# Gates of two mixing branches as seven block products ahead of the attention, and attention heads that overlap at their ends

## The chip, the core and the metric

The kernel runs on one core of a Trainium2 chip. The metric is the time of one execution in device microseconds (us). A core has five engines with an instruction stream each: TensorE (PE in the profile) multiplies matrices, VectorE (DVE) and ScalarE (ACT) work elementwise, GpSimd (POOL) copies, fills and issues some transfers, SyncE (SP) issues most transfers. Each engine takes its instructions in order and waits on semaphores for the others.

## The reference

Two layers, each a feed-forward half step, a gated mixing of three branches, and another feed-forward half step, on 512 tokens of 1024 features in float32. The change is in the mixing:

```
u = _rmsnorm(h, mix_pre_g[l])
proj = u @ w_in[l]
q_sb, k_sb, v_sb, q_fx, k_fx, v_fx, f_logit, q_mem = jnp.split(proj, split_at, axis=-1)
o_sb  = _stick_breaking_attention(...)      # 8 heads of 64
o_fx  = _forgetting_attention(...)          # 8 heads of 64
o_mem = _memory_attention(...)              # 4 heads of 128
g_sb, g_fx, g_mem = jnp.split(jax.nn.sigmoid(u @ w_gate[l] + b_gate[l]), N_BRANCH, axis=-1)
merged = (g_sb * (_merge_heads(o_sb) @ w_br_sb[l])
          + g_fx * (_merge_heads(o_fx) @ w_br_fox[l])
          + g_mem * (_merge_heads(o_mem) @ w_br_mem[l]))
h = h + _rmsnorm(merged @ w_out[l], mix_post_g[l])
```

Both causal attentions multiply queries by keys (scores `z`), turn them to weights by chains of exponentials, and multiply these by the values.

## The kernel before

Every matrix product in float32 is done as three matmuls (`mm3`, L212-216). Each factor is split into a high half, a cast on ACT (L188, or L191 with a scale), and the rest, a subtraction on DVE (L189, L192); the product is high x high, high x low and low x high. Tiles with an h or l in the name (`wh_`, `wl_`) are these halves.

A weight unit (`Unit`) is half a megabyte: SP loads it into a `raw` buffer (L262; four buffers), ACT and DVE split it into a `wh` and a `wl` tile (four of each, used in a ring). Work for PE is kept as jobs in a queue `Q`; a job loads its units, and units of later jobs are loaded and split ahead. Attention heads are generators ("chains") that `Q.weave` interleaves with jobs: a chain yields the PE time it has emitted and a time that it wants to wait, and jobs fill the waits. So the order of the program is set by these written times, and the engines follow it.

The feed-forward parts use a scheme of block products in place of the plain one: a product of 2 x 2 blocks by 2 x 2 blocks is done as seven products (n = 0 to 6) with sums of blocks as factors. Such units are `BlockUnit`s: products 2 and 5 have a sum of two weight blocks, built in a buffer `kt` by one load on SP and an adding load on POOL (L317); products 3 and 6 add a third block to the same buffer on DVE (L343). Factors on the token side that are sums are `ag_2` to `ag_5`. The `kt` buffers of the feed-forward groups are of the tag `v`, which has six.

In the mixing part of a layer `us_a` holds the normalised tokens, already split. Order: keys and values of the memory (`pmk`, `pmv`), queries of the memory heads (`pqm_0` to `pqm_3`, tile `qm`), four memory heads (scores `zm`, transposes `ptm`, values `pvm`), then for each pair of heads the projections (`pq`, `pk`, `pv`) and eight stick-breaking heads (scores `zs`, weights `ts`, transposes `pts`, values `pvs`, branch 0), and eight forgetting heads (`zf`, `pf`, `ptf`, `pvf`, branch 1). What fills the waits is merging: for each branch and quarter of the features `merge` runs the gate's product (bank `pg`, weights `wg`), the sigmoid as a chain of five steps on ACT and DVE (tile `ga`, L202-210), the branch's own product (bank `pb`, weights `wb`), and adds to `mg`. Gates are computed directly before they are used, with 512 tokens as the moving side:

```
pg = pbank("mm", "pg" + nm)
products = gemm(pg[:], ug, m, act)
```

## Time and profile before

| | |
|---|---|
| runs, us | 2353.73, 2354.14, 2354.50 (median 2354.14) |
| profiled execution, span from first to last instruction, us | 2352.7 |
| instructions | 30543 |
| TensorE busy, us | 2342.4 |
| VectorE busy, us | 1779.2 |
| ScalarE busy, us | 1453.0 |
| GpSimd busy, us | 213.4 |
| bytes moved, mean | 366.46 MB, 156 GB/s |

The profiled execution is known by its span alone; the runs, which take in what lies ahead of the first and behind the last instruction, are 1.0 to 1.8 us longer. Busy times are sums of the rows of an engine. A matmul's row lasts from its issue to the modelled end of its result, and the next is issued before that, so rows overlap; what a stream of matmuls costs is read from the distance of their starts. In group rows the columns are line, engine, operation, output and inputs, shape and count, then busy us and mean ns of one, then idle time of the engine just before and what ended it. In rows of a timeline they are start and length in us. Wait rows give the engine, its instruction, what it waited for, us in total, times, and the longest.

### The profile page before, as it was taken

What the parts mean: (1) busy time and instruction counts of PE and PEld (TensorE: products, weight loads), DVE (VectorE), ACT (ScalarE), POOL (GpSimd) and SP (SyncE); (2) the same over time, 40 slices, a digit from 0 to 9 for tenths busy, and PEclk for the clock granted to TensorE, in tenths of its full rate; (3) what the DMA queues carried; (4) which work ended last, traced back from release to release, by engine and by line L of the source; (5) the groups of instructions that cost most, each with busy time, mean ns of one, the idle gap of its engine ahead of it and who ended that gap; (6) DMA issues with size and microseconds to landing.
All of it is one profiled execution on the core that took longest, in us unless ns stands there. A gap on an engine that the chain in (4) does not pass through costs nothing.

```text
span 2352.7 us, 30543 instructions
## 1 busy us (share of the span) xinstructions
PE 2342.4 (100%) x11368; PEld 1970.4 (84%) x11368; DVE 1779.2 (76%) x2423; ACT 1453.0 (62%) x2347; POOL 213.4 (9%) x242
## 2 busy tenths in 40 slices
PE   9999999999999999999999999999999999999998
PEld 8888888888888888888888888888888888888887
DVE  8766977678776687768887679766877766866696
ACT  6665765576665565566665566656776655655574
POOL 1101100001120011101011110000011100111100
PEclk9999999999999999999999999999999999999999
DMA  8866854222323476659586767532222234776682
GB/s 249 234 180 173 230 181 142 72 73 81 88 66 116 153 221 173 179 158 258 174 215 170 187 186 232 190 101 81 72 82 81 72 126 153 223 182 176 179 224 98
DMA packets 233112, 366.46 MB, mean 156 GB/s; under 512 B 11242, under 2 KB 101634, under 8 KB 232452
## 3 DMA queue, kind: packets, MB, share of 16 engines
q1 hardware_dynamic: 202400, 305.76, 40.2%
q0 software_dynamic: 30560, 58.76, 14.5%
q8 instruction: 89, 1.46, 0.3%
q14 instruction: 59, 0.48, 0.1%
q10 hardware_dynamic: 4, 0.00, 0.0%
HBM read 349.80 MB, written 14.68 MB: 155 GB/s over the span
## 4 chain that ended last, share of the span: by engine, by line
PE 60%; DVE 0%; issue 0%; ACT 0%; DVEq 0%
PE ptc L214 5%; PE ptc L216 5%; PE ptc L215 5%; PE pdc L214 3%; PE pdc L216 3%; PE pdc L215 3%; PE pta L214 3%; PE pta L216 3%; PE pta L215 3%; PE pg L214 2%; PE pg L215 2%; PE pg L216 2%; PE pda L215 2%; PE pda L216 2%; PE pda L214 2%; PE pb L216 1%
## 5 line engine op out<-in xcount | busy, mean ns | idle before, releaser
L214 PE MATMUL pg<-us_a,wh_wg 128*128 128x512 f32 x384 | 150.9, 393 | 0.0
L216 PE MATMUL pg<-us_a,wl_wg 128*128 128x512 f32 x384 | 149.6, 390 | 0.0
L215 PE MATMUL pg<-us_a,wh_wg 128*128 128x512 f32 x384 | 149.5, 389 | 0.0
L189 DVE TENSOR_TENSOR wl_tc<-ktc,wh_tc 128x1024 fp32r<-128x1024 f32 x80 | 97.7, 1224 | 63.6 <-ACT wh_tc L188 63.6
L189 DVE TENSOR_TENSOR wl_ta<-kta,wh_ta 128x1024 fp32r<-128x1024 f32 x80 | 97.6, 1224 | 58.4 <-ACT wh_ta L188 58.4
L188 ACT CAST wh_tc<-ktc 128x1024 fp32r<-128x1024 f32 x80 | 84.1, 1054 | 68.0 <-PE ptc L216 47.8
L216 PE MATMUL pta<-wh_ta,aga 128*128 128x512 f32 x320 | 124.7, 390 | 1.2 <-DVE aga L189 1.2
L214 PE MATMUL ptc<-wh_tc,agc 128*128 128x512 f32 x320 | 125.4, 393 | 0.1
L214 PE MATMUL pta<-wh_ta,aga 128*128 128x512 f32 x320 | 125.2, 392 | 0.0
L216 PE MATMUL ptc<-wh_tc,agc 128*128 128x512 f32 x320 | 124.7, 390 | 0.0
L215 PE MATMUL ptc<-wl_tc,agc 128*128 128x512 f32 x320 | 124.6, 389 | 0.0
L188 ACT CAST wh_ta<-kta 128x1024 fp32r<-128x1024 f32 x80 | 84.2, 1053 | 65.5 <-PE pta L216 41.7
L215 PE MATMUL pta<-wl_ta,aga 128*128 128x512 f32 x320 | 124.6, 389 | 0.0
L189 DVE TENSOR_TENSOR wl_tc<-raw_tc,wh_tc 128x1024 fp32r<-128x1024 f32 x56 | 68.5, 1224 | 45.4 <-ACT wh_tc L188 45.4
L189 DVE TENSOR_TENSOR wl_ta<-raw_ta,wh_ta 128x1024 fp32r<-128x1024 f32 x58 | 70.9, 1224 | 42.0 <-ACT wh_ta L188 41.9
L188 ACT CAST wh_ta<-raw_ta 128x1024 fp32r<-128x1024 f32 x58 | 60.9, 1052 | 45.6 <-PE pta L216 38.0
L188 ACT CAST wh_tc<-raw_tc 128x1024 fp32r<-128x1024 f32 x56 | 59.0, 1054 | 48.1 <-PE ptc L216 36.6
L214 PE MATMUL ptc<-wh_tc,us_b 128*128 128x512 f32 x224 | 87.6, 391 | 0.2
L214 PE MATMUL pda<-wh_da,aa 128*128 128x512 f32 x224 | 87.5, 391 | 0.0
L214 PE MATMUL pdc<-wh_dc,ac 128*128 128x512 f32 x224 | 87.5, 391 | 0.0
L216 PE MATMUL ptc<-wh_tc,us_b 128*128 128x512 f32 x224 | 87.2, 389 | 0.0
L215 PE MATMUL ptc<-wl_tc,us_b 128*128 128x512 f32 x224 | 87.2, 389 | 0.0
(559 smaller groups left out, 7417.1 us busy)
## 6 DMA issues: line engine op xcount, KB each, us to landing
raw_wg<-in_w_gate_dram SPq DMA_DIRECT2D x48, 512.0 KB, 3.6
raw_ta<-in_ffn_w_gate_dram SPq DMA_DIRECT2D x44, 512.0 KB, 4.3
raw_tc<-in_ffn_w_gate_dram SPq DMA_DIRECT2D x44, 512.0 KB, 4.6
raw_da<-in_ffn_w_down_dram SPq DMA_DIRECT2D x42, 512.0 KB, 3.9
raw_dc<-in_ffn_w_down_dram SPq DMA_DIRECT2D x42, 512.0 KB, 3.9
kta<-in_ffn_w_up_dram SPq DMA_DIRECT2D x40, 512.0 KB, 6.1
ktc<-in_ffn_w_up_dram SPq DMA_DIRECT2D x40, 512.0 KB, 5.7
raw_wo<-in_w_out_dram SPq DMA_DIRECT2D x24, 512.0 KB, 3.7
```

The costliest lines, as they stand in the source:

```text
L188: both = [nc.scalar.copy(h_ap, src)]
L189: make = lambda: nc.vector.tensor_tensor(l_ap, src, h_ap.bitcast(F32), ALU.subtract)
L214: nc.tensor.matmul(pt, lh, rh, start=start, stop=False, skip_group_check=free)
L215: nc.tensor.matmul(pt, lh, rl, start=False, stop=False, skip_group_check=free)
L216: nc.tensor.matmul(pt, ll, rh, start=False, stop=stop, skip_group_check=free)
```

## The change

For branches 0 (stick-breaking) and 1 (forgetting) the gate is no longer computed at the merge. The product `w_gate` x tokens is done as seven block products, features on the output's partitions and 256 tokens on the moving side (`block_gates`). Product 0 of both branches and product 1 of branch 0 stand ahead of the memory queries, the rest (2 to 6 of branch 0, then 2, 3, 4, 5, 1, 6 of branch 1) behind them and ahead of the causal heads. `settle` takes the sigmoid with ACT's own function (which needs an activation table of its own, loaded there and put back behind) and stores the gate to DRAM (`gsave`, a DMA of ACT's queue); `merge` reads it back by a DMA of POOL's queue. The memory branch's gate stays as it was (`mem_gate`), and its own product stands in a job apart (`mem_branch`). The factors `ag_2`, `ag_3` are tiles of the tag `tri`, `ag_4h`, `ag_4l`, `ag_5h`, `ag_5l` of the tag `o`, as are the sums of weight blocks `kt`; `o` has eight buffers, as before. `block_units`, `seeds` and the token sums (`input_sums`) were moved to the top, so that both users share them.

The causal heads are one chain (`causal`): when a head has emitted its transposes, the next head's chain is started 3 us later (`W_NEXT`), so that its scores stand ahead of the previous head's values. The table of extra waiting times by head (`W_MORE`) is gone.

```
+        def factor(n):
+            if n < 4:
+                t = stile([P, 2, 4, S // 2], "tri", f"ag{l}_{n}")
+                return t[:, 0], t[:, 1]
+            return tuple(stile([P, 4, S // 2], "o", f"ag{l}_{n}{x}")[:] for x in "hl")
...
+        def settle(br, i, j, banks=None):
+            t = st.pop(("c", i, j))
+            for m in range(4):
+                c = HALVES[m % 2]
+                d = br * ND + 4 * j + m
+                nc.scalar.activation(t[:, m // 2, c], t[:, m // 2, c] if banks is None else banks[m // 2][:, c], AF.Sigmoid,
+                                     bias=nbgate[:, l, d:d + 1], scale=-1.0 if j else 1.0)
+            nc.scalar.dma_start(gsave[br, i, j], t[:].rearrange("p e q -> p (e q)"))
+
+        def block_gates(br, n, uns, top):
...
+            if n in (0, 1, 2) and not seeded:
+                st["gb", SUM[n]] = [pbank("mm", f"{nm}_{n}_{e}") for e in range(2)]
+            pts = st.pop(("gb", 1)) if n == 1 else st["gb", SUM[n]]
+            opens, ends = n in (0, 1, 2) and not seeded, n in (1, 4, 6)
+            for un in uns:
+                for k in range(un.nk):
+                    kk = un.k0 + k
+                    for m in range(4):
+                        c = slice(m * P, (m + 1) * P)
+                        mm3(pts[m // 2][:, HALVES[m % 2]], un.h[:, k, c], un.l[:, k, c], *tokens(n, kk),
+                            opens and kk == 0 and m % 2 == 0, ends and kk == ND // 2 - 1 and m % 2 == 1, free=True)
+                        yield 3 * S // 2 * PE_US
...
+            for e in range(2):
+                if n in (2, 3):
+                    nc.scalar.copy(t[:, e], pts[e][:])
+                elif n in (4, 5):
+                    nc.vector.tensor_tensor(t[:, e], t[:, e], pts[e][:], ALU.add)
...
+            if n not in (2, 3):
+                settle(br, i, j, None if n in (4, 5) else pts)
...
-                    if br == 2:
-                        nc.vector.tensor_tensor(md, a[:], pb[:], ALU.mult)
-                    else:
-                        nc.vector.tensor_tensor(a[:], a[:], pb[:], ALU.mult)
-                        nc.vector.tensor_tensor(md, md, a[:], ALU.add)
+                    nc.vector.tensor_tensor(a[:], a[:], pb[:], ALU.mult)
+                    nc.vector.tensor_tensor(md, md, a[:], ALU.add)
...
+        todo, made = [], None
+        for br, order in zip(SETS, (FIRST, ORDER)):
+            keep = Keep(lambda i, k0, br=br: stile([P, 2, S], "o", f"kt{l}_{br}_{i}_{k0}", F32)[:])
+            made, rounds = block_units(order, keep, ND // 2, f"wg{l}_{br}", w_gate[l][:, br * D:(br + 1) * D], made)
+            top = max((1, 4), key=order.index)
+            todo.append([(uns, lambda br=br, n=n, uns=uns, top=top: block_gates(br, n, uns, top)) for n, uns in rounds])
+        Q.add(*todo[0].pop(0), src.ready((0, 1)))
+        Q.add(*todo[0].pop(0))
+        Q.add(*todo[1].pop(0))
...
+            def causal(n):
...
+                for kind, us_ in begun.pop(n, None) or head_of(n):
+                    yield kind, us_
+                    steps += kind == "pe"
+                    if kind == "pe" and steps == 2 and n + 1 < 2 * NH:
+                        Q.spawn(causal(n + 1), W_NEXT)
```

How the instructions stand now. TensorE behind the last memory queries, in layer 0: before, the first head's projection and the memory heads follow (`pqm_3` is the last query product, `pvm_0` the values of the first memory head):

```order
L216 MATMUL pqm_3_3477<-us_a_1_3056,wl_qm_1_4_3278 128x512
L214 MATMUL pq_0_0_3552<-us_a_0_3055,wh_q_0_0_3313 128x512
L215 MATMUL pq_0_0_3552<-us_a_0_3055,wh_q_0_0_3313 128x512
L216 MATMUL pq_0_0_3552<-us_a_0_3055,wl_q_0_0_3314 128x512
L214 MATMUL pvm_0_3556<-ptm_0_3516,mv_0_3307 128x512
```

Now the products of the gates stand there first. This is TensorE where branch 0 goes over to branch 1 (`g_0_0` and `g_1_2` are banks by branch and sum; `wh_wg_1_3_0` is the weight unit of branch 1, product 3, first half):

```order
L216 MATMUL g_0_0_1_3705<-us_a_1_3057,wh_wg_0_6_2_3834 128x256
L217 MATMUL g_0_0_1_3705<-us_a_1_3057,wh_wg_0_6_2_3834 128x256
L218 MATMUL g_0_0_1_3705<-us_a_1_3057,wl_wg_0_6_2_3835 128x256
L216 MATMUL g_1_0_0_4034<-ag_3_3611,wh_wg_1_3_0_3959 128x256
L217 MATMUL g_1_0_0_4034<-ag_3_3611,wh_wg_1_3_0_3959 128x256
L216 MATMUL g_1_0_1_4035<-ag_3_3611,wh_wg_1_3_0_3959 128x256
L217 MATMUL g_1_0_1_4035<-ag_3_3611,wh_wg_1_3_0_3959 128x256
L216 MATMUL g_1_2_0_4038<-ag_2_3528,wh_wg_1_2_0_3895 128x256
L217 MATMUL g_1_2_0_4038<-ag_2_3528,wh_wg_1_2_0_3895 128x256
```

Four matmuls of product 3 of branch 1 come directly behind product 6 of branch 0, and product 2 behind them. VectorE at the same place: before, splits of the value weights and work of the memory heads:

```order
L189 TENSOR_TENSOR wl_v_0_2_3432<-raw_v_0_2_3281,wh_v_0_2_3431 128x1024
L189 TENSOR_TENSOR qm_3_3549<-pqm_3_3477,qm_3_3549 128x512
L189 TENSOR_TENSOR om_0_3385<-pvm_0_3556,om_0_3385 128x512
L1386 TENSOR_REDUCE stm_2_0_3572<-zm_2_0_3565 128x2
L1386 TENSOR_REDUCE stm_2_1_3588<-zm_2_1_3581 128x2
```

Now (`cg` collects a quarter of the gates; L1622 empties a bank into it; L345 adds the third block to the sum):

```order
L191 TENSOR_TENSOR wl_wg_0_6_0_3828<-kt_0_0_0_3326,wh_wg_0_6_0_3827 128x1024
L1622 TENSOR_TENSOR cg_0_01_3823<-cg_0_01_3823,g_0_2_0_3708 128x512
L1622 TENSOR_TENSOR cg_0_01_3823<-cg_0_01_3823,g_0_2_1_3709 128x512
L191 TENSOR_TENSOR wl_wg_0_6_2_3835<-kt_0_0_2_3329,wh_wg_0_6_2_3834 128x1024
L1622 TENSOR_TENSOR cg_0_11_3758<-cg_0_11_3758,g_0_0_0_3704 128x512
L191 TENSOR_TENSOR wl_wg_1_2_0_3896<-kt_1_0_0_3690,wh_wg_1_2_0_3895 128x1024
L1622 TENSOR_TENSOR cg_0_11_3758<-cg_0_11_3758,g_0_0_1_3705 128x512
L191 TENSOR_TENSOR wl_wg_1_2_2_3900<-kt_1_0_2_3699,wh_wg_1_2_2_3899 128x1024
L345 TENSOR_TENSOR kt_1_0_0_3690<-kt_1_0_0_3690,raw_wg_1_3_0_3693 128x1024
L345 TENSOR_TENSOR kt_1_0_2_3699<-kt_1_0_2_3699,raw_wg_1_3_2_3702 128x1024
```

The split of `kt_0_0_2` for product 6 of branch 0 and the splits of `kt_1_0_0` and `kt_1_0_2` for product 2 of branch 1 now follow each other there. SyncE, behind the loads of the query weights, before:

```order
L262 DMA raw_qm_1_4_3151<-in_w_in_dram 128x4x256
L262 DMA raw_q_0_0_3209<-in_w_in_dram 128x8x128
L262 DMA raw_k_0_0_3215<-in_w_in_dram 128x8x128
L262 DMA raw_v_0_0_3275<-in_w_in_dram 128x2x512
L262 DMA raw_v_0_2_3281<-in_w_in_dram 128x2x512
```

and now, where the buffers of `kt_1_0_0` and `kt_1_0_2` are those that `kt_0_0_0` and `kt_0_0_2` held:

```order
L319 DMA raw_wg_1_3_0_3693<-in_w_gate_dram 128x2x512
L319 DMA raw_wg_1_3_2_3702<-in_w_gate_dram 128x2x512
L319 DMA raw_wg_1_1_0_3831<-in_w_gate_dram 128x2x512
L319 DMA raw_wg_1_1_2_3838<-in_w_gate_dram 128x2x512
L319 DMA kt_1_0_0_3690<-in_w_gate_dram 128x2x512
L319 DMA kt_1_0_2_3699<-in_w_gate_dram 128x2x512
L319 DMA kt_1_1_0_3765<-in_w_gate_dram 128x2x512
L319 DMA kt_1_1_2_3772<-in_w_gate_dram 128x2x512
L264 DMA raw_q_0_0_4026<-in_w_in_dram 128x8x128
L264 DMA raw_k_0_0_4032<-in_w_in_dram 128x8x128
```

The loads of the first head's weights moved behind those of the gates. TensorE between the first two stick-breaking heads, before:

```order
L1278 MATMUL pvs_0_0_4010<-pts_0_0_3959,v_0_0_3780 128x512 x2
L1278 MATMUL pvs_0_0_4010<-pts_0_0_3959,v_0_1_3808 128x384 x2
L1278 MATMUL pvs_0_0_4010<-pts_0_0_3959,v_0_2_3872 128x256 x2
L1278 MATMUL pvs_0_0_4010<-pts_0_0_3959,v_0_3_3909 128x256 x2
L1305 MATMUL zs_0_1_3_4024<-k_0_0_3743,q_0_0_3689 128x512 x2
L1305 MATMUL zs_0_1_2_4025<-k_0_0_3743,q_0_0_3689 128x384 x2
L1305 MATMUL zs_0_1_1_4026<-k_0_0_3743,q_0_0_3689 128x256 x4
```

and now:

```order
L1307 MATMUL zs_0_1_3_5031<-k_0_0_4572,q_0_0_4495 128x512 x2
L1307 MATMUL zs_0_1_2_5032<-k_0_0_4572,q_0_0_4495 128x384 x2
L1307 MATMUL zs_0_1_1_5033<-k_0_0_4572,q_0_0_4495 128x256 x4
L1280 MATMUL pvs_0_0_5067<-pts_0_0_4990,v_0_0_4609 128x512 x2
L1280 MATMUL pvs_0_0_5067<-pts_0_0_4990,v_0_1_4749 128x384 x2
L1280 MATMUL pvs_0_0_5067<-pts_0_0_4990,v_0_2_4837 128x256 x2
L1280 MATMUL pvs_0_0_5067<-pts_0_0_4990,v_0_3_4874 128x256 x2
```

The scores of the second head moved ahead of the values of the first. Lines of the changed kernel are 2 higher at this place (L1305 is now L1307, L262 now L264, L317 now L319, L189 now L191, L343 now L345).

More of the change, by code (lines that the diff above doesn't have):

```diff
@@ L1363, in fox_head @@
             ptile[i] = p
+        ahead()
         yield ("pe", 1.5)
@@ new lines, in merge, with run @@
+        def merge(br, w_br, dp):
+            ub = wpair(w_br[l], NP, dp * 256, f"wb{l}_{br}_{dp}")
+            def run():
+                gate = []
+                for m in range(2):
+                    d = 2 * dp + m
+                    gate.append(tmp(f"ga{l}_{br}_{d}"))
+                    c = slice(d % 4 * S // 2, (d % 4 + 1) * S // 2)
+                    nc.gpsimd.dma_start(gate[m][:].rearrange("p (i q) -> p i q", i=2),
+                                        gsave[br, :, d // 4, :, c].rearrange("i p q -> p i q"))
@@ L1650, in run @@
         def run():
-            Q.until(marks["first"])
-            for i in range(NT):
-                nc.sync.dma_start(hsave[i], hT[i][:])
+            Q.until(marks["sets"])
             st["o", 2] = [blk("o", f"om{l}_{i}") for i in range(NMH)]
@@ new lines, in causal @@
+            def causal(n):
+                if n % 2 == 0:
+                    Q.past(marks[heads[n // 2]], W_K, Q.limit)
+                if n == 0:
+                    Q.until(marks["v"])
+                if n == NH:
+                    Q.until(marks["mem"])
+                    st["o", 1] = [blk("o", f"o{l}_1_{p}") for p in range(NP)]
+                steps = 1 if n in begun else 0
+                for kind, us_ in begun.pop(n, None) or head_of(n):
[3 more added lines that the diff above has]
+                        Q.spawn(causal(n + 1), W_NEXT)
+                if n % 2 == 1 and n + 1 < 2 * NH:
+                    Q.limit = limits[n // 2 + 1]
```

296 lines of the change are left out of this document (163 added, 133 removed).

## The prediction

> **What bounds the kernel now.** I read the page's busy times first, then the clock, the waits of TensorE, and the mixing phase alone.
>
> ```profile
> span 2352.7 us, 30543 instructions
> PE 2342.4 (100%) x11368; PEld 1970.4 (84%) x11368; DVE 1779.2 (76%) x2423; ACT 1453.0 (62%) x2347; POOL 213.4 (9%) x242
> ...
> PEclk9999999999999999999999999999999999999999
> ...
> PE 60%; DVE 0%; issue 0%; ACT 0%; DVEq 0%
> ```
>
> ```profile
> PE warm L1733 <- DVE warm L1817: 1.3, 1, 1.3
> PE pta L216 <- DVE aga L189: 1.2, 1, 1.2
> PE ptf L1291 <- DVE pf L1362: 0.7, 2, 0.4
> ```
>
> ```profile
> 420.00:640.00 220.00, 219.63 (x1160) 189.12 (x1159) 169.25 (x273) 148.50 (x273) 23.09 (x36) 1.00 0.27 77
> 640.00:760.00 120.00, 120.00 (x612) 101.97 (x611) 89.14 (x177) 70.12 (x140) 13.16 (x22) 1.00 0.31 97
> ```
>
> PE (TensorE) is busy for 2342.4 of 2352.7 us, at full clock, and all its waits for other engines come to 3.2 us (second fence). The stretches of the third fence are attention and merging of the first layer: PE busy for 219.63 of 220 us and 120 of 120. So two things alone can move the time: the number and size of matmuls, and new waits of PE. Whatever the change takes from DVE (76%) and ACT (62%) is worth nothing by itself, and I cost the removed exponentials and maxima of 32 gates at zero, since PE covers them.
>
> **Part 1, the matmuls.** Plain gates of branches 0 and 1 take 2 layers x 2 branches x 8 feature blocks x 8 contraction blocks x 3 = 768 of the 1152 matmuls in the three `pg` groups. The changed kernel has 2 x 2 x 7 products x 16 x 3 = 1344 matmuls of 256 columns in their stead. A matmul's duration in a row is latency that overlaps its neighbour's; what counts is the distance from start to start:
>
> ```profile
> 422.14 0.39 PE L214 MATMUL pv<-wh_v,us_a 128*128 128x512 f32 x1
> ...
> 424.86 0.39 PE L214 MATMUL pv<-wh_v,us_a 128*128 128x512 f32 x1
> ```
>
> ```profile
> 351.79 0.28 PE L215 MATMUL pmk<-mn,wh_mk 128*128 128x256 f32 x1
> ...
> 352.99 0.28 PE L216 MATMUL pmk<-mn,wl_mk 128*128 128x256 f32 x1
> ```
>
> Between the first two rows lie 12 steps, 2.72 / 12 = 0.227 us for 512 columns; between the other two 10 steps, 1.20 / 10 = 0.120 us for 256. 768 x 0.227 = 174.3; 1344 x 0.120 = 161.3; the term is **-13.0 us**. The other matmuls stay as they were. Seven eighths of the arithmetic would give 174.3 / 8 = 21.8, but a half-size matmul costs 0.120 and not 0.1135, so 40% of that is lost.
>
> The Trainium skill, "TensorE: Matmul & The Clock Gate", section "Wait — 56ns, not 53.3ns?", has the distance as N / 2.4 GHz plus about 2.5 ns once warm. An estimate from it is 215.7 ns for 512 and 109.2 ns for 256 columns, so 165.7 - 146.8 = 18.9 us saved instead of 13.0. The two rows above speak against it: 227 and 120 ns fit a fixed part of some 13 ns per matmul.
>
> **Part 2, loading of weights for the products.** The plain gate needed whole blocks only. Products 2 and 5 multiply by a sum of two blocks, which is built in a buffer `kt` by a load on SP and a second, adding load on POOL; products 3 and 6 add a third block to the same buffer on DVE. The same scheme runs in the feed-forward groups of before, so its prices are there:
>
> ```profile
> ktc<-in_ffn_w_up_dram SPq DMA_DIRECT2D x40, 512.0 KB, 5.7
> ktc<-in_ffn_w_gate_dram POOLq DMA_DIRECT2D x20, 512.0 KB, 7.3
> raw_tc<-in_ffn_w_gate_dram SPq DMA_DIRECT2D x44, 512.0 KB, 4.6
> raw_wg<-in_w_gate_dram SPq DMA_DIRECT2D x48, 512.0 KB, 3.6
> ```
>
> ```profile
> L188 ACT CAST wh_tc<-ktc x80: 1042/1055/1062, 877.6 to 2224.6; 128x1024 fp32r<-128x1024 f32 x80
> L189 DVE TENSOR_TENSOR wl_tc<-ktc,wh_tc x80: 1216/1225/1226, 878.9 to 2225.7; 128x1024 fp32r<-128x1024 f32 x80
> ...
> L343 DVE TENSOR_TENSOR ktc<-ktc,raw_tc x40: 1217/1224/1227, 881.1 to 2204.2; 128x1024 f32<-128x1024 f32 x40
> ...
> DMA to landing us min/median/max: 4.5/6.7/10.6
> ```
>
> ```profile
> 888.47 0.46 SPq L317 DMA_DIRECT2D ktc<-in_ffn_w_up_dram  x1
> ...
> 901.33 0.37 SPq L317 DMA_DIRECT2D ktc<-in_ffn_w_up_dram  x1
> ```
>
> ```profile
> 893.65 1.20 POOL L317 DMA_DIRECT2D ktc<-in_ffn_w_gate_dram  x1 [14.52 <-DMA ktc<-in_ffn_w_up_dram]
> ```
>
> ```profile
> 900.07 1.23 DVE L189 TENSOR_TENSOR wl_tc<-ktc,wh_tc 128x1024 fp32r<-128x1024 f32 x1 [1.45 <-ACT wh_tc L188]
> ```
>
> The last rows show the hand-overs: the split that frees a buffer ends at 901.30 and SP issues at 901.33; an SP load issued at 888.47 lets POOL's adding load start 5.2 us later. In the feed-forward groups `kt` has six buffers of its own and product 0 of the next group stands between product 6 of one and product 2 of the next. In the gate stage it gets four of the eight `o` buffers (the other four hold the factors of products 4 and 5), and product 0 of branch 1 has been moved far ahead. So `kt_1_0_0` and `kt_1_0_2`, which branch 1 needs for products 2, 3 and 6, can load only when branch 0 has split its sums for product 6, and PE goes from product 6 of branch 0 straight to products 3 and 2 of branch 1.
>
> I count from the end of product 4 of branch 0 on PE (T = 0). Products 5 and 6 and two matmuls of a memory head follow, 98 x 0.120 = 11.8 us; then the first matmuls of product 3 are due. Against that: the ring of four `wh` tiles lets the cast for the second half of product 6 start when product 4 has left PE, at 0.3 (a 256-column row lasts 0.28); cast 1.05 and split 1.22 end at 2.6. SP's load of `kt_1_0_2` lands 5.7 later, POOL takes some 0.6 to start, the adding load takes 7.3: 16.2. Then ACT casts (1.05), DVE splits (1.22), DVE adds the block for product 3 (1.22, behind that split on its engine), ACT casts again (1.05), with 0.2 for hand-overs 4.7: 20.9. PE was due at 11.8 and stands in order, so **9.1 us** by the medians. Lower end: both loads at the 4.5 us that is the shortest `ktc` landing, no start-up: 2.6 + 9.0 + 4.7 - 11.8 = 4.5. Upper end: one load at the longest landing, 10.6: 12.4. I take 8.3, nearer to the median than to the minimum: plain loads in the mixing phase meet less traffic than in the groups (`raw_wg` 3.6 against `raw_tc` 4.6), though the products themselves will add to it. PE would already stop for part of this within product 6, since DVE's split for `kt_1_0_0` is ahead of the addition that empties a bank of product 5; that is the same time, not more. Nothing gives it back, as PE has no idle time behind it. Two layers: **+16.6 us** (9.0 to 24.8).
>
> The Trainium skill, "DMA: Bandwidth & Descriptors", section "Anatomy of one DMA — SWDGE (gpsimd) path", fits such a POOL transfer as 2.0 us plus bytes / 436e3. An estimate by it is 3.2 us for 512 KB, and the term would be 2 x 5.0 = 10.0 us instead of 16.6. The row says 7.3, over twice that, in the same scheme; I keep the row.
>
> What else waits behind these: SP's loads of `kt_1_1`, then of the first head's q and k, stand behind `kt_1_0` on the queue, all needed 17 us of PE or more later. POOL's queue has only these adding loads there, since its copies for the heads come behind. Branches 0 and 1 now have 14 splits each and layer instead of 8, and four additions: 12 x 1.05 = 12.6 us more on ACT and 20 x 1.22 = 24.4 on DVE in a layer, all in the gate stage. Its PE time is 14 x 5.76 = 81 us with the queries' 22 besides; both engines, at 62% and 76% before, still fit there, and both lose the gates' exponentials later.
>
> **Part 3, parked gates and table loads.** Eight stores per layer on ACT's queue, sixteen reads on POOL's, and two activation tables per layer:
>
> ```profile
> L774 ACT ACT_TABLE_LOAD x4 | 5.1, 1283 | 0.1
> ```
>
> ```profile
> hsave<-ha SPq DMA_DIRECT2D x8, 512.0 KB, 3.9
> ```
>
> A table is 1.28 us on ACT, 62% busy; a half-megabyte takes 3.9 us to park, and all eight heads of branch 0 lie between a store and its reading. The reads are issued when the branch's weights are at hand and behind POOL's copies for heads; I put 0.3 us per layer on the first ones of branch 0, and between 0 and 2.
>
> **Part 4, overlapped heads.** Score products `zs` of the next head now stand ahead of the value products `pvs` of the previous one. Before, an even and an odd head follow each other:
>
> ```profile
> 520.67 1.46 PE L1305 MATMUL zs<-k,q 128*128 128x512 f32 x8
> 534.23 1.25 PE L1291 MATMUL pts<-ident,ts 128*128 128x128 f32 x10
> 540.11 1.44 PE L1278 MATMUL pvs<-pts,v 128*128 128x512 f32 x8
> ```
>
> ```profile
> L1322 ACT ACTIVATE ts<-ts x3: 526/526/632, 528.0 to 532.8; 128x384 f32<-128x384 f32 x2, 128x512 f32<-128x512 f32 x1
> ```
>
> From the end of `zs` (522.1) to the transposes PE has 12.1 us of other work, and the head's last exponential ends at 533.3, 0.9 before them. By the pitches the order after leaves 10.8 to 13.2 us there, so one or two heads per layer come short by a few tenths. Odd heads of branch 0 have their first value product hoisted to 0 to 3 us behind the transposes; it needs one cast only, of some 0.6 us: 0.4 us at each of three heads. At the end the products of the last branch come straight after the last head's output, where before a gate stood between: 1 us. Against that go the stalls of the old order, 0.4 to 0.7 us as the waits show. With part 3 I take **+1.5 us** for both layers. Ends: -2, if heads come without wait, and +7, if twelve hoisted or short heads of both layers lose 0.6 us each.
>
> **The sum.** The profiled execution spans 2352.7 us, 1.4 under the median of the runs, 2354.14. 2352.7 - 13.0 + 16.6 + 1.5 = 2357.8, and 1.4 around it: **2359 us**, 0.2% slower. A measurement of this kernel tells 0.2% (4.7 us) from no change, so this lies at the edge of what can be told.
>
> **Rivals.** *A, the round trip is hidden* (faster). If the adding load of `kt_1_0_2` lands soon enough, PE goes through; the limit is 11.8 - 4.7 = 7.1 us after product 4, that is two loads in 4.5 us together. No `ktc` row has that, but it happens if the buffers come free earlier than I read or PE reaches product 4 late. With 0 to 3 us left per layer: 2354.1 - 13.0 + 1.5 + (0 to 6) = 2343 to 2349. *B, the heads lose more* (slower). If the chain of exponentials is later by 1 us in each of the eight stick-breaking heads, because ACT now has the splits and the next head's scores in between, 16 us come on top: 2367 to 2376. For it: the 0.9 us of slack above; against: ACT and DVE have lost the gates' exponentials in that stretch. *C, half hidden*: a wait of 3 to 6 us per layer gives 2349 to 2355. *D, a half-size matmul costs half*: with 0.227 / 2 for 256 columns the 1344 take 152.5 us and the term is -21.8, so 2350. The pitch of 0.120 in the `pmk` rows speaks against it; nothing else in the gate products differs from those. The Trainium skill's formula in part 1 goes that way: with its 18.9 the sum is 2353.
>
> **How the numbers follow.** Forecast as summed, waits of 6 to 12 us per layer (2354 to 2367): 0.52. A: 0.16. B: 0.14. C: 0.12. D: 0.06. About two fifths of the forecast, four fifths of C and all of D lie within 0.2%, 2349.4 to 2358.8: 0.21 + 0.10 + 0.06 = 0.37. Faster is A with the rest of C: 0.18. Slower: 0.31 + 0.14 = 0.45. The range goes from within A to within B, 2347 to 2370; the forecast's own is 2354 to 2367.
>
> **What would show it.** Right: in each layer one idle time of PE of 6 to 12 us, ahead of or inside product 6 to 2 of the gates, put down to ACT or DVE and behind them to POOL's load; PE's busy time down by some 13 us; 1344 rows with a pitch of 0.120. Wrong: no such gap (A), gaps before transposes or value products of branch 0 (B), or another pitch (D).

## The result: 1.3% slower, and the profile after

The changed kernel takes 2385.89 us (2384.80 to 2386.35) against 2354.32 for the kernel before, 1.0134 times as long (95% interval 1.0119 to 1.0148). I had forecast 2359, with a range to 2370: the sign was right, the size was not. The head of the page after:

```profile
span 2383.1 us, 32064 instructions
...
PE 2348.5 (99%) x11944; PEld 1992.8 (84%) x11944; DVE 1828.6 (77%) x2443; ACT 1484.0 (62%) x2404; POOL 254.3 (11%) x290
...
PE 88%; DVE 5%; issue 2%; DMA 2%; ACT 2%; POOL 0%; DVEq 0%; SPq 0%; POOLq 0%; ACTq 0%
```

TensorE is still 99% busy, yet the chain that ended last now passes through DVE, DMA and ACT for 9% of the span; before, none of the three had 1% of it (that chain accounts for 60% of the span). PE's waits in the after trace (us in total, times, longest), largest first:

```profile
PE g L216 <- ACT wh_wg L190: 6.4, 2, 3.7
PE pb L216 <- DVE ga L1674: 5.9, 2, 3.1
PE zf L1351 <- DVE ptf L191: 3.1, 6, 1.3
PE g L216 <- DVE cg L1622: 2.3, 2, 1.7
PE zs L1307 <- POOL cs L1453: 2.0, 2, 1.0
PE pvs L1280 <- ACT pts L190: 1.8, 2, 0.9
```

These six sum to 21.5 us, which less the 13 saved would be +8.5. To see the rest I took, from the whole trace, every matmul's distance to the next start less the usual distance of its shape (0.227, 0.175, 0.120 and 0.109 us for 512, 384, 256 and 128 columns, 0.056 for the masks in bfloat16) and summed this **lost time** over three stretches of a layer: gates and memory heads; from the first scores of a causal head to the first value product of the seventh forgetting head ("heads"); from there to the output projection ("end"). Lost time is of the one profiled execution of a kernel, time and interval are of all its runs. Both layers, in us:

| kernel | gates | heads | end | time | ratio to before, interval |
|---|---|---|---|---|---|
| before | 0.4 + 0.1 | 1.7 + 1.7 | 0.0 + 0.0 | 2354.3 | |
| after | 6.9 + 8.0 | 8.6 + 9.4 | 6.9 + 6.7 | 2385.9 | 1.0134, 1.0119 to 1.0148 |
| e1_kt_buffers | 19.5 + 18.8 | 8.5 + 11.3 | 7.2 + 7.4 | 2411.6 | 1.0240, 1.0223 to 1.0257 |
| e1b_kt_of_product_2 | 0.4 + 0.7 | 8.3 + 9.3 | 6.7 + 7.4 | 2370.2 | 1.0071, 1.0056 to 1.0086 |
| e2_reads_early | 5.7 + 6.3 | 8.4 + 9.4 | 3.2 + 3.3 | 2379.2 | 1.0101, 1.0086 to 1.0117 |
| e4_heads_in_turn | 7.1 + 7.0 | 12.5 + 14.0 | 9.5 + 8.4 | 2395.9 | 1.0176, 1.0161 to 1.0191 |
| e5_three | 19.4 + 19.1 | 12.5 + 14.2 | 9.4 + 8.8 | 2421.9 | 1.0286, 1.0271 to 1.0302 |
| e6_heads_alone | 0.4 + 0.1 | 7.4 + 7.4 | 0.1 + 0.1 | 2366.8 | 1.0053, 1.0038 to 1.0068 |
| e7_blocks_of_branch_1 | 0.4 + 0.3 | 7.5 + 7.6 | 0.1 + 0.1 | 2360.8 | 1.0027, 1.0016 to 1.0038 |
| e7_blocks_of_branch_0 | 0.4 + 0.7 | 8.3 + 8.5 | 5.9 + 6.3 | 2372.3 | 1.0076, 1.0059 to 1.0092 |
| e8_limit | 0.4 + 0.1 | 3.7 + 3.7 | 0.1 + 0.1 | 2358.8 | 1.0018, 1.0008 to 1.0027 |
| e8_limit_and_later | 0.4 + 0.1 | 4.6 + 4.6 | -0.1 - 0.1 | 2360.5 | 1.0025, 1.0015 to 1.0036 |
| e9_two_repairs | 0.4 + 0.4 | 8.3 + 9.2 | 3.3 + 4.2 | 2363.6 | 1.0040, 1.0027 to 1.0053 |
| e10_branch_1_repaired | 0.4 + 1.2 | 4.7 + 4.9 | 0.0 + 0.0 | 2354.6 | 1.0001, 0.9991 to 1.0010 |
| e11_reads_off_ring | 0.4 + 0.4 | 7.2 + 7.2 | 3.0 + 3.1 | 2360.4 | 1.0027, 1.0016 to 1.0037 |
| e11_all_repairs | 0.4 + 0.4 | 3.4 + 3.4 | 7.6 + 5.1 | 2358.9 | 1.0019, 1.0011 to 1.0028 |
| e12_branch_1_in_turn | 0.4 + 0.4 | 1.9 + 1.9 | 0.6 + 0.6 | 2349.6 | 0.9979, 0.9971 to 0.9988 |
| e13_branch_1_limit | 2.2 + 0.3 | 3.9 + 3.9 | 0.1 + 0.1 | 2353.1 | 0.9993, 0.9984 to 1.0002 |

After less before is 14.4 in the gates, 14.6 in the heads, 13.6 at the end: 42.6. Less the 13 of the smaller matmuls that is 29.6; the spans differ by 30.4. So three losses of like size; I had foreseen the first and put 1.5 on the other two together.

**Gates.** Where branch 0 goes over to branch 1, in the first layer, on DVE, SP, POOL, ACT and PE:

```profile
425.65 1.23 DVE L191 TENSOR_TENSOR wl_wg<-kt,wh_wg 128x1024 fp32r<-128x1024 f32 x1 [1.61 <-ACT wh_wg L190]
428.53 1.23 DVE L191 TENSOR_TENSOR wl_wg<-kt,wh_wg 128x1024 fp32r<-128x1024 f32 x1 [1.65 <-ACT wh_wg L190]
431.41 1.23 DVE L191 TENSOR_TENSOR wl_wg<-kt,wh_wg 128x1024 fp32r<-128x1024 f32 x1 [1.65 <-ACT wh_wg L190]
432.61 1.41 DVE L1622 TENSOR_TENSOR cg<-cg,g 128x512 f32<-128x512 f32 x2
434.30 1.23 DVE L191 TENSOR_TENSOR wl_wg<-kt,wh_wg 128x1024 fp32r<-128x1024 f32 x1 [0.28 <-ACT wh_wg L190]
```

```profile
426.91 9.01 SPq L319 DMA_DIRECT2D kt<-in_w_gate_dram  x4
...
429.79 6.13 SPq L319 DMA_DIRECT2D kt<-in_w_gate_dram  x3
```

```profile
431.57 1.21 POOL L319 DMA_DIRECT2D kt<-in_w_gate_dram  x1 [18.59 <-DMA kt<-in_w_gate_dram]
434.10 1.20 POOL L319 DMA_DIRECT2D kt<-in_w_gate_dram  x1 [1.33 <-DVE cg L1622]
```

```profile
438.88 1.05 ACT L190 CAST wh_wg<-kt 128x1024 fp32r<-128x1024 f32 x1 [2.52 <-DMA kt<-in_w_gate_dram]
...
445.07 1.05 ACT L190 CAST wh_wg<-kt 128x1024 fp32r<-128x1024 f32 x1 [4.66 <-DMA kt<-in_w_gate_dram]
...
448.60 1.05 ACT L190 CAST wh_wg<-kt 128x1024 fp32r<-128x1024 f32 x1 [0.87 <-DVE kt L345]
```

```profile
441.84 0.38 PE L216 MATMUL g<-us_a,wh_wg 128*128 128x256 f32 x1 [0.61 <-DVE cg L1622]
449.70 0.38 PE L216 MATMUL g<-ag,wh_wg 128*128 128x256 f32 x1 [3.65 <-ACT wh_wg L190]
```

SP's four loads start at 426.91, just as the split begun at 425.65 ends, and the second at 429.79, when that of 428.53 ends. In VectorE's order the two additions of L1622 stand between product 6's two splits, so these are the ones at 431.41 and 434.30, and the two before them are product 5's: the words of the part on the change and of part 2, that `kt_1_0` takes over the buffers of product 6's sums, were mistaken. The first adding load, issued at 431.57, has landed at 438.9, 7.3 us later; the second is issued at 434.10 and what ACT waits for lands at 445.0, nearly 11 us later. Whether it was held up by the first or by the other transfers there, no run tells. Then cast, split, addition and cast take 4.7 us, and PE resumes at 449.70.

**End.** Around the last forgetting head, on POOL, DVE and PE:

```profile
786.21 2.89 POOL L1665 DMA_DIRECT2D ga<-gsave  x4 [11.43 <-PE ptf L1293]
```

```profile
792.25 0.69 DVE L1674 TENSOR_TENSOR ga<-ga,pb 128x512 f32<-128x512 f32 x1 [3.90 <-DMA ga<-gsave]
```

```profile
793.00 0.80 PE L216 MATMUL pb<-o,wh_wb 128*128 128x512 f32 x1 [3.15 <-DVE ga L1674]
793.59 0.63 PE L217 MATMUL pb<-o,wh_wb 128*128 128x512 f32 x1
794.02 0.63 PE L218 MATMUL pb<-o,wl_wb 128*128 128x512 f32 x1
795.07 1.01 PE L1280 MATMUL pvf<-ptf,v 128*128 128x256 f32 x3 [0.42 <-DVE ptf L191]
...
800.06 0.39 PE L216 MATMUL pb<-o,wh_wb 128*128 128x512 f32 x1
800.29 0.39 PE L217 MATMUL pb<-o,wh_wb 128*128 128x512 f32 x1
```

POOL issues the reads of parked gates only after the head's transposes: their tiles come from the ring of five temporary tiles (`tmp`) that the heads' weights fill. The edit e2 below tests this. VectorE stands in order behind the read for 3.9 us, and the splits of the last head's weights, queued behind it, are late for PE.

### The profile page after: what moved, and what is told of

It is laid out like the page before. It is cut to its first block, busy times and chain, and to the rows that moved or that the text cites. A ratio compares the mean times of both kernels' runs of the same rounds, so it can differ in the third digit from the quotient of the medians.

```text
span 2383.1 us, 32064 instructions
## 1 busy us (share of the span) xinstructions
PE 2348.5 (99%) x11944; PEld 1992.8 (84%) x11944; DVE 1828.6 (77%) x2443; ACT 1484.0 (62%) x2404; POOL 254.3 (11%) x290
## 4 chain that ended last, share of the span: by engine, by line
PE 88%; DVE 5%; issue 2%; DMA 2%; ACT 2%; POOL 0%; DVEq 0%; SPq 0%; POOLq 0%; ACTq 0%
PE ptc L216 5%; PE ptc L218 5%; PE ptc L217 5%; PE pta L216 5%; PE pta L218 5%; PE pta L217 5%; PE pdc L218 3%; PE pdc L216 3%; PE pda L217 3%; PE pda L218 3%; PE pdc L217 3%; PE pda L216 3%; PE g L216 2%; PE g L217 2%; PE g L218 2%
## 5 line engine op out<-in xcount | busy, mean ns | idle before, releaser
L191 DVE TENSOR_TENSOR wl_tc<-ktc,wh_tc 128x1024 fp32r<-128x1024 f32 x80 | 97.7, 1223 | 63.3 <-ACT wh_tc L190 63.3
L191 DVE TENSOR_TENSOR wl_ta<-kta,wh_ta 128x1024 fp32r<-128x1024 f32 x80 | 97.5, 1222 | 57.6 <-ACT wh_ta L190 57.6
L191 DVE TENSOR_TENSOR wl_ta<-raw_ta,wh_ta 128x1024 fp32r<-128x1024 f32 x58 | 70.9, 1223 | 44.0 <-ACT wh_ta L190 43.9
L191 DVE TENSOR_TENSOR wl_tc<-raw_tc,wh_tc 128x1024 fp32r<-128x1024 f32 x56 | 68.5, 1224 | 45.4 <-ACT wh_tc L190 45.4
L216 PE MATMUL pda<-wh_da,aa 128*128 128x512 f32 x224 | 87.5, 391 | 0.0
L218 PE MATMUL pda<-wh_da,aa 128*128 128x512 f32 x224 | 87.2, 389 | 0.0
L217 PE MATMUL pda<-wl_da,aa 128*128 128x512 f32 x224 | 87.2, 389 | 0.0
L217 PE MATMUL pdc<-wl_dc,ac 128*128 128x512 f32 x224 | 87.2, 389 | 0.0
```

The lines of the kernel that those rows point to most:

```text
L191: make = lambda: nc.vector.tensor_tensor(l_ap, src, h_ap.bitcast(F32), ALU.subtract)
L216: nc.tensor.matmul(pt, lh, rh, start=start, stop=False, skip_group_check=free)
L217: nc.tensor.matmul(pt, lh, rl, start=False, stop=False, skip_group_check=free)
L218: nc.tensor.matmul(pt, ll, rh, start=False, stop=stop, skip_group_check=free)
```

## The experiments

**e1_kt_buffers.** Sums of branch 1 in the tag `v`.

```
-            keep = Keep(lambda i, k0, br=br: stile([P, 2, S], "o", f"kt{l}_{br}_{i}_{k0}", F32)[:])
+            keep = Keep(lambda i, k0, br=br: stile([P, 2, S], "ov"[br], f"kt{l}_{br}_{i}_{k0}", F32)[:])
```

> The changed kernel with one edit: the sums of weight blocks of branch 1 lie in buffers of the tag v, free at that place, instead of those that branch 0's sums have to leave first. Order of the program unchanged. In the trace of the changed kernel TensorE loses 6.7 and 7.8 us (stalls and the slow matmuls behind them) where branch 0's product 6 goes over to branch 1. Theory (the buffers' round trip makes this wait): both go, under 1 us left per layer, 2386 - 14 = 2372 us (2370 to 2375). Rival (ACT and DVE cannot split fast enough there, or the loads themselves are late for want of bandwidth): most of the wait stays, 2382 to 2387.

25 us slower, outside what theory and rival had. PE had no wait at the change of branches, but SP issued `kt_1_1` at 466 and PE waited for it in product 5 (the `g` row of the waits, 5.5 at the longest):

```profile
466.27 14.45 SPq L319 DMA_DIRECT2D kt<-in_w_gate_dram  x2
```

```profile
PE g L216 <- ACT wh_wg L190: 13.2, 4, 5.5
PE ptm L1408 <- DVE pm L1398: 10.9, 4, 3.3
```

The edit brought waits of its own, in the memory heads too (`ptm`), so it decides between neither. **e1b_kt_of_product_2** moves only `kt_1_0`:

```
-            keep = Keep(lambda i, k0, br=br: stile([P, 2, S], "o", f"kt{l}_{br}_{i}_{k0}", F32)[:])
+            keep = Keep(lambda i, k0, br=br: stile([P, 2, S], "v" if (br, i) == (1, 0) else "o", f"kt{l}_{br}_{i}_{k0}", F32)[:])
```

> The changed kernel with one edit, narrower than the first try: of branch 1's sums of weight blocks only those for products 2, 3 and 6 (kt_1_0) lie in the tag v, those for product 5 stay in the tag o. In the first try the wait at the change of branches was gone, but kt_1_1 issued at 466 instead of 432 us, behind whatever held its new buffers, so TensorE waited later. Theory (the round trip of kt_1_0's buffers makes the 6.7 and 7.8 us): they fall under 2 us per layer and nothing new comes, 2386 - 12 = 2374 us (2370 to 2378). Rival (loads and splits there are too slow anyway, a gain at one place is lost at the next): 2382 or more.

15.7 us faster than the change, and the gates lose 0.4 and 0.7. That the weight sums wait for buffers, and that this costs all of the first loss, is shown.

**e2_reads_early.** Branch 1's gates are read into tiles of the tag `o`, one job ahead.

```
-                    gate.append(tmp(f"ga{l}_{br}_{d}"))
...
+                    for n in range(dp, min(dp + 2, ND // 2)):
+                        if ("ga", n) not in st:
+                            st["ga", n] = stile([P, 2, S], "o", f"ga{l}_{br}_{n}", F32)
```

> The changed kernel with one edit: the gates of branch 1 are read back into buffers of the tag o (left by branch 0's head outputs) instead of the ring of five temporary tiles that the heads use too, and each pair is read one job ahead. In the trace TensorE loses 6.9 and 6.7 us at the last head, where a read was issued at 786.2 behind the heads' transposes and VectorE waited for it in order. Theory (the reads are late because of the ring and GpSimd's order, and block VectorE): these go to under 2 us per layer, 2386 - 10 = 2376 us (2373 to 2378). Rival (the last head's own chain of weights and values is what TensorE waits for, the read only lies beside it): less than 4 us gained in all, 2382 or more.

6.7 us faster, between theory and rival; the end falls from 13.6 to 6.5. So about half of the loss at the end was these reads. The profiled execution is the fastest of this kernel, 3.9 us under the median (2375.3 to 2379.6 in its runs), so the stretches flatter it a little.

**e4_heads_in_turn.** The next head starts when a head is done.

```
-                    if kind == "pe" and steps == 2 and n + 1 < 2 * NH:
-                        Q.spawn(causal(n + 1), W_NEXT)
...
+                if n + 1 < 2 * NH:
+                    Q.spawn(causal(n + 1))
```

> The changed kernel with one part undone: a head starts only when the one before has emitted its values, as before the change; gates as changed. In the trace of the changed kernel the stretch of the heads up to the last one loses 8.6 us in the first layer and 9.1 in the second, where the kernel before lost under 2. Theory (the overlap itself makes these waits: hoisted value products and scores meet banks and casts that are not ready): 2386 - 14 = 2372 us (2368 to 2376). Rival (they come from the missing gates, which used to fill the waits of the heads, and from POOL's reads): with heads in turn there is still too little beside them, the loss stays or grows, 2383 to 2395.

10 us slower, just above the rival's range. Each second stick-breaking head now waits for its cast, and the last forgetting head for its exponentials:

```profile
PE ptf L1293 <- DVE pf L1365: 13.0, 4, 6.2
PE pvs L1280 <- ACT pts L190: 12.5, 8, 1.8
```

But the heads do not stand here as they stood before the change. The table `W_MORE` is still missing, and so is something that neither the part on the change nor the prediction names: the limit up to which a head may take jobs from the queue. Before, each of the two heads of a pair had its own, the second head's a pair further on (`limits[p][j]` in the edit of e12 below, p for the pair and j for the head); the changed kernel has one for both and raises it when the second head is done. So in e4, as in the changed kernel, a second head can run out of jobs between its transposes and its values. This is the first second head of the changed kernel:

```profile
565.75 1.25 PE L1293 MATMUL pts<-ident,ts 128*128 128x128 f32 x10
567.88 0.50 PE L1280 MATMUL pvs<-pts,v 128*128 128x512 f32 x1 [0.88 <-ACT pts L190]
```

Before the change the first second head had 3.3 us of other work there (its transposes start at 470.69 and last 1.25, its first value product starts at 475.21). So e4 shows that heads in turn with the narrower limit are worse than overlapped ones; it does not show that overlap helps. **e5_three** put the edits of e1_kt_buffers, e2 and e4 together.

> The three edits together: own buffers for the sums of branch 1, gates of branch 1 read early into buffers of their own, heads in turn. Left of the change are the smaller matmuls of the gates (13 us fewer by the pitches) and the parked gates of both branches. Theory (the three losses are separate and each edit takes away its own): 2386 - 14 - 10 - 14 = 2348 us (2343 to 2355), faster than before. Rival (the losses cover one another, a wait that goes is taken up by the next): 2358 to 2370.

2421.9 us, far from both: the gates lose what they lose in e1_kt_buffers and the heads what they lose in e4. The end loses 18.2 where e4 lost 17.9, so the early reads, worth 7 us there with overlapped heads, are worth nothing while PE waits for the last head's exponentials.

**e6_heads_alone.** Overlapped heads as changed, all gates plain as before; `merge` computes the gate of a branch that is not in `SETS`.

```
-    SETS = (0, 1)
+    SETS = ()
...
+            def gates():
+                for m in range(2):
...
+                    yield from gemm(pg[:], ug, m, act)
+                    sigmoid_neg(own[m][:], pg[:], nbgate[:, l, br * ND + d:br * ND + d + 1])
```

> Only the other half of the change: heads overlapped at their ends as in the changed kernel, all gates computed plainly at the merge as before (no block products, no parked gates, no second activation table). Theory F (the heads' waits in the changed kernel come from the gates that no longer stand between the steps of the heads as work for TensorE): with them back the heads lose under 4 us per layer, and the time is that of before, 2354 us (2350 to 2358). Rival O (the overlapped order itself waits): 2354 + 14 = 2368 us (2362 to 2374).

12.4 us slower than before, 11.4 of it in the heads: rival O's number. So with the gates' work in place the other half of the change is a loss by itself. That half is the overlap with the narrower limit, the missing table and the memory branch's own jobs; e8 parts the limit from the rest.

**e7_blocks_of_branch_1** and **e7_blocks_of_branch_0** make block products of one branch (`SETS = (1,)`, with early reads, or `(0,)`).

> Block products for branch 1 alone, parked, and read early into buffers of their own; branch 0's gates plain at their merge as before; heads overlapped. Half of the smaller matmuls: 2 x 336 in place of 2 x 192 long ones, 6.5 us fewer by the pitches. No sums of a second branch, so no round trip of kt buffers. Branch 0's gates stand among the forgetting heads again. Theory F: 2354 - 6.5 + 3 = 2350 us (2346 to 2356). Rival O (the overlap loses 7 us per layer whatever stands between): 2362 (2357 to 2366).

> Block products for branch 0 alone, parked and read at the merge through the ring of temporary tiles; branch 1's gates plain at their merge, behind the heads; heads overlapped. The same 6.5 us fewer, no round trip of kt buffers, and nothing read at the last merge. But the forgetting heads lack branch 0's gates as work between their steps. Theory F: the forgetting heads lose 3 to 5 us per layer, the end nothing, 2354 (2350 to 2360), some 4 us slower than with the blocks of branch 1. Rival O: as with branch 1, 2362, no difference between the two.

Branch 1 alone, 2360.8 us: the matmuls' gain of half the change and the heads' loss of e6, nothing else, as rival O had it. Branch 0 alone, 2372.3 us, is outside both ranges: the end, where theory F had no loss, loses 12.2. There DVE again stands behind a read and PE's `pvf` behind DVE:

```profile
737.02 1.44 POOL L1681 DMA_DIRECT2D ga<-gsave  x2 [11.43 <-PE ptf L1293]
```

```profile
743.37 0.69 DVE L1706 TENSOR_TENSOR ga<-ga,pb 128x512 f32<-128x512 f32 x1 [4.22 <-DMA ga<-gsave]
```

```profile
PE pvf L1280 <- DVE ptf L191: 7.3, 2, 4.5
```

**e8_limit** (on e6): jobs of the next pair may be taken once a pair's second head has its scores out. **e8_limit_and_later** also has `W_NEXT = 3.5`.

```
-                if n % 2 == 1 and n + 1 < 2 * NH:
-                    Q.limit = limits[n // 2 + 1]
...
+                    if kind == "pe" and steps == 1 and n % 2 == 1 and n + 1 < 2 * NH:
+                        Q.limit = limits[n // 2 + 1]
```

> The heads alone (plain gates, overlapped heads: 2366.8 us, 12.4 over the kernel before) with one edit: jobs of the next pair of heads may be taken as soon as a pair's second head has emitted its scores, not only when that head is done. By the order of instructions each second head then has 4.7 us of other work between its transposes and its values, where there were 0 to 3, and 12.9 us between its scores and transposes, where the next head had 10.8. Theory L (the queue of jobs ran dry for the second head of a pair): the waits of pvs on a cast (1.0 us per layer) and of pts on the last exponential (0.4) go with the slow matmuls behind them, 2362 us (2360 to 2364); the waits of zs and zf stay. Rival Z (all of it comes from the banks of tag z, which transposes and the next scores share): no change, 2366 (2365 to 2368).

> The same, and the next head starts 3.5 us after the transposes instead of 3.0, so that by the order its scores come 4.1 us behind the transposes and not 3.4. Theory L and Z together: scores wait for a bank of tag z until ACT and DVE have split the transposes out of it (in the trace zf stands 2.8 us behind the transposes of the last stick-breaking head, and its first split starts 2.1 us behind them); with 0.7 us more these waits shrink, 2358 us (2355 to 2361). Rival (the wait is bound to what ACT and DVE do at that place and moves along): within 1.5 us of the run without this edit.

The limit is worth 8.0 us, more than theory L expected: the waits of `pvs` went (1.8 in e6), and with them those of `zs` and `zf` that theory L left standing; the wait of `pts` on the last exponential stayed (0.6, now 0.8). The edit gives the second head back about the reach that it had before the change, so two thirds of the heads' loss in e6 (7.4 of 11.4) come from the narrower limit and not from the overlap. It repeats: with the blocks of branch 1 the limit is worth 7.7 (e7 to e13 below). Starting later brought nothing (+1.7, the intervals overlap): that the shared banks make the remaining 2 us per layer is not shown. With the later start PE's waits for DVE on `zs` were these; without it there were none:

```profile
PE zs L1306 <- DVE pts L190: 3.6, 4, 1.1
```

**e9_two_repairs** joins e1b and e2; **e10_branch_1_repaired** puts both edits of e8 on the blocks of branch 1.

> The changed kernel with two repairs at once: kt_1_0 in the tag v (alone: -15.7 us) and branch 1's gates read early into buffers of their own (alone: -6.7). Heads overlapped as changed. Theory (separate losses): 2386 - 15.7 - 8 = 2362 us (2359 to 2366), what is left over the smaller matmuls being the heads' waits, 17 us. Rival (they cover one another): 2368 or more.

> Block products for branch 1 alone, gates read early (2360.8 us), with the two edits to the heads (limit, 3.5 us). If the heads' loss is as theories L and Z have it, some 9 of 13 us go: 2352 us (2349 to 2355), at or a little under the kernel before. Rival (heads lose as much as before these edits): 2359 or more.

Both as expected, e10 2.6 us above its centre; so the losses of the gates and of branch 1's reads are separate. In e9, 7.5 us at the end remain: POOL's queue has branch 0's reads, through the ring, ahead of branch 1's:

```profile
777.27 7.23 POOL L1662 DMA_DIRECT2D ga<-gsave  x10 [11.40 <-PE ptf L1293]
```

**e11_reads_off_ring** gives branch 0's reads a tile of their own (tag `gr`, one buffer); **e11_all_repairs** adds the limit of e8.

```
-                    gate = [tmp(f"ga{l}_{br}_{2 * dp + m}")[:] for m in range(2)]
+                    gate = [sb.tile([P, S], F32, tag="gr", bufs=1, name=f"ga{l}_{br}_{2 * dp}")[:], None]
```

> The changed kernel with the two repairs (2363.6 us) and one more: branch 0's gates are read back into one tile of their own instead of the ring of five temporary tiles, one feature block at a time. Theory R (late reads: in the run with two repairs POOL waits 11.4 us for the transposes of the last head before it can issue branch 0's reads, branch 1's are queued behind them, and VectorE waits in order): the 4.0 us per layer at the last head go, 2363.6 - 7 = 2357 us (2354 to 2359). Rival F (too little work is left between the steps of the last heads): 2361 or more, the waits of pvf stay and are put down to ACT or DVE's splits.

> The same with the queue's limit raised (worth 8.0 us with the heads alone). If the causes named so far are all and add up: 2357 - 8 = 2349 us (2346 to 2352), under the kernel before, with the smaller matmuls' 13 us less some 8 us of waits of zs and zf and at the end. Rival F (the heads need the gates as work): raising the limit uses up work sooner that is then missing at the last heads, 2354 to 2360.

The first gains 3.2, half of what theory R had and between it and the rival: 3.1 fewer lost in the heads and 1.4 at the end. It does not take the reads out of PE's way. With one buffer a read must wait until the block before it has been used, and PE's longest waits are still behind a read:

```profile
PE pb L216 <- DVE ga L1686: 4.3, 2, 2.2
DVE ga L1686 <- DMA ga<-gsave: 14.0, 8, 4.3
```

The second gains 7.6 in the heads and loses 6.6 at the end, in rival F's range. PE's waits there are for a cast, a bank and the last head's output:

```profile
775.58 0.50 PE L1280 MATMUL pvf<-ptf,v 128*128 128x512 f32 x1 [0.94 <-ACT ptf L190]
780.05 0.50 PE L216 MATMUL pb<-o,wh_wb 128*128 128x512 f32 x1 [1.43 <-DVE ga L1686]
783.36 0.80 PE L216 MATMUL pb<-o,wh_wb 128*128 128x512 f32 x1 [1.40 <-DVE sf L1284]
```

The first and the third fit the rival: too little other work. The second is again a read, since the DVE row that ends it (779.31) waited 1.30 us for `ga<-gsave`. So how much of the end is want of work and how much late reads of branch 0 stays open.

**e12_branch_1_in_turn** has blocks for branch 1 alone, read early, and the heads exactly as before the change; **e13_branch_1_limit** is e7 of branch 1 with the limit.

```
-    SETS = (0, 1)
-    W_NEXT = 3.0
+    SETS = (1,)
+    W_MORE = {(0, 0): (-8.0, -1.5), (0, 1): (-0.7, -1.0), ...}
...
-            Q.weave(causal(0), limits[0])
+                for j in range(2):
+                    Q.weave(begun.pop((p, j), None) or stick(p, j), limits[p][j])
```

> Block products for branch 1 alone, its gates read early; branch 0 and memory gates and the whole order of the heads as in the kernel before (heads in turn, table of waiting times). The overlap's waits are gone, the smaller matmuls bring 6.5 us, reading at the last merge costs about 1: 2349 us (2347 to 2351), faster than both kernels. Rival (the heads need branch 1's first gates, that stood beside the last heads, as work): 2353 or more.

> Block products for branch 1 alone with overlapped heads and the queue's limit raised, next head at 3.0 us. With 3.5 us it took 2354.6; with the heads alone 3.0 was 1.7 better than 3.5: 2353 us (2351 to 2355). If overlapped heads are as good as heads in turn once the queue holds, it equals the run before this one, 2349; the difference between the two is what the shared z banks cost.

e12 takes 2349.6 us, 4.9 or 0.2% under the kernel before: faster than both kernels, as expected, and 6.5 for the matmuls less some 2 lost. Its rival falls: the last heads do without branch 1's first gate as work. e13 takes 2353.1, as expected too. The 3.5 us between them, nearly all in the heads, are the price of overlap, missing table and order of the memory branch's jobs together; no run parts these, so that it is the shared `z` banks is not shown. PE's waits of e12, all that are over 0.1 us in sum and lie in the mixing:

```profile
PE ptf L1294 <- DVE pf L1365: 0.7, 2, 0.4
PE pb L217 <- DVE sf L1285: 0.3, 2, 0.2
```

## Why the prediction was wrong, step by step

- **Part 1, the matmuls (-13.0): right.** The `g` rows stand 0.120 apart:

```profile
430.01 0.28 PE L217 MATMUL g<-ag_4l,wh_wg 128*128 128x256 f32 x1
...
431.93 0.28 PE L218 MATMUL g<-ag_4h,wl_wg 128*128 128x256 f32 x1
```

  16 steps in 1.92 us. The estimate of 18.9 from the Trainium skill ("TensorE: Matmul & The Clock Gate", section "Wait — 56ns, not 53.3ns?") and rival D fall; the blocks of branch 1 alone brought about half of 13 (6.0 between e6 and e7, 5.7 between e8 and e13).
- **Part 2, loading (+16.6): right in mechanism, and near in size by luck.** The loss is 14.4, or 15.7 by e1b, but two misses stand against each other. The buffers came free with product 5, so SP's second load started at 429.79 and not at 435.5, when product 6's second split ended; against that the adding load took 11 us and not 7.3. PE stood still for 0.8 and 3.8 us in the first layer, not 8.3, and 1.9 us more went in slow matmuls. The loads of `kt` in the gate stage landed later than in the groups, where the median was 6.7:

```profile
DMA to landing us min/median/max: 4.0/8.1/15.2
```

  The Trainium skill's fit for such a transfer ("DMA: Bandwidth & Descriptors", section "Anatomy of one DMA — SWDGE (gpsimd) path"), by which I had estimated 3.2 us for 512 KB, is further off here than in the row of before.
- **Part 3, parked gates (+0.3 per layer): the step that failed.** I priced the reads as transfers and said that they stand "behind POOL's copies for heads", but did not ask what their tiles wait for, nor what stands on VectorE behind the multiplication that uses them. The end lost 13.6: reads of branch 1 are 7 of it (e2), the rest is reads of branch 0 and want of work at the last head, not parted. Reads of branch 0 cost another 3 in the heads (e11).
- **Part 4, heads (+1.5 with part 3): the other.** It lost 14.6. I read 0 to 3 us between a second head's transposes and its first value product from the order and costed 0.4 us at three heads; the trace has 1.0 us at the first, and the other waits of the first layer's heads are mostly of scores (`zs`, `zf`), ten of them over 0.15 us, 6.0 us together. The term was mis-sized, and its cause misread: I took the 0 to 3 us for a trait of the overlap, but they come from the narrower limit of the queue. The rows of before in part 4 could not show it, since they are of one head, the fifth, which is the first of its pair. That limit is 7.4 to 8.0 us (e6 to e8, e7 to e13, the heads of e11), the reads of branch 0 are 3 (e11), and the overlap with the missing table leaves about 4. The sum is near rival B's 16 us by chance; the cause is another than B names: work for PE was out of reach within a pair.
- **What I costed at nothing.** "PE covers them" was said of the removed gates' exponentials; the other side, that the removed matmuls were PE's cover for the heads, I had as a remark on the last head only. It mattered less than e4 had made me think: with the limit back, the heads lose 6.8 without these gates (e11_all_repairs) and 7.4 with them (e8). At the end it may matter (12.7 lost in e11_all_repairs), but there late reads are mixed in.

## What to carry to other kernels

Work fills a wait only if the program may reach it there: when the order of steps is rewritten, compare for each step which work it could take before and which now, not only how much work there is. Here a limit that looked like bookkeeping cost more than the overlap. A value parked in memory comes back through a queue, a buffer and an in-order engine; each of the three can make a read of 4.5 us (the median of `ga<-gsave`) into a stop of PE, and the buffer must not be from a ring that the waiting work fills. If a gain is in one half of a change and the loss in the other, try the halves: the blocks of one branch with the old order of heads kept 4.9 of 6.5 us. The blocks of both branches with that old order, limit and table were not run.

## What the runs showed that I had not expected

After a stop of 3 to 4 us PE runs at half clock for some microseconds. The columns below are the stretch in us, its length, PE busy (count), granted clock, DMA share and GB/s, of the after trace, first at the end and then in the gates:

```profile
789.00:793.00 4.00, 0.85 (x6) 0.88 0.88 327
793.00:796.00 3.00, 2.58 (x7) 0.50 0.81 253
796.00:799.00 3.00, 3.00 (x8) 0.52 1.04 408
799.00:802.00 3.00, 3.00 (x15) 1.00 0.45 150
...
450.00:454.00 4.00, 4.00 (x21) 0.59 1.06 235
```

The `pb` rows of the end have 0.43 us from 793.59 to 794.02 and 0.23 from 800.06 to 800.29. So a 3.2 us wait there cost nearly 7 with the waits that follow at that clock. The Trainium skill, "TensorE: Matmul & The Clock Gate", section "What's actually happening", says that the array falls to half clock after an idle window of about 3.4 us and needs about as long of busy time to come back; the trace agrees as to the half clock (0.50 and 0.52), but here it lasted 6 us and followed 3.2 us of idleness. Nor is one long stop needed: in e11_all_repairs the three waits shown above, none over 1.5 us, lie within 8 us, and from 784 to 787 us the granted clock is 0.50. In this kernel a stop of PE had to be priced with what followed it: about half as much again for the gates, twice for the end.
